# Masks of two attentions' logits written by VectorE instead of TensorE, with products of the side chains held behind the projections, in a two-layer mixer trunk

## The chip, the cores and the metric

One core of one Trainium2 chip runs the whole program. The metric is the device time of one execution in microseconds, as the median of several executions; the kernel before takes 605.12 us (three runs, 604.92 to 605.28). Engines are named as the profile names them: PE is TensorE's matrix multiplication, PEld its loads of the stationary operand, DVE is VectorE, ACT is ScalarE, POOL is GpSimd, SP issues the DMAs.

## What is computed

Two layers of a pre-norm mixer on 256 frames of width 1024. One wide projection feeds three token mixers: a gated linear attention (A), a sparse attention whose keys a token indexer picks (B), and a differential attention (C). Sigmoid gates merge them and an output projection adds the result to the residual stream. Cut to what matters:

```python
for l in range(DEPTH):                                    # 2 layers, T = 256, D = 1024
    h = rms(x, norm_g[l])
    gq, gk, gv, ga, gz, bq, bk, bv, iq, ik, iw, bz, cq, ck, cv, cz, gate = split(h @ w_in[l])
    y_a = gla(gq, gk, gv, ga, ...) * silu(gz)
    # B: score = sum_h iw[h] * relu(iq[h] . ik); the 64 best admissible keys of each query are kept
    #    p = softmax(where(kept, q . k, -inf)); o = p @ v
    y_b = dsa(bq, bk, bv, iq, ik, iw, ...) * silu(bz)
    # C: two maps a head; a query sees the keys up to the end of its chunk of 64 frames
    #    p_c = softmax(where(allowed, q_c . k_c, -inf)); o = (p_0 - lam * p_1) @ v
    y_c = diff(cq, ck, cv, ...) * silu(cz)
    g = sigmoid(gate.reshape(B, T, 3, D))
    x = x + (g0 * (y_a @ w_br[0]) + g1 * (y_b @ w_br[1]) + g2 * (y_c @ w_br[2])) @ w_out[l]
```

## The kernel before

Every product in float32 precision is made of three products of a high and a low part (`mm3`, L191 to L194: high by high, high by low, low by high). Weights arrive in units of 128 x 1024 (`raw`, five buffers); ACT rounds a unit to its high part `whi` and DVE subtracts to the low part `wlo` (L148; six buffers of each). The projections are the bulk of PE's work: for each name of `ORDER` (`bq`, `cq`, `ck`, `gate2`, ... `br0`, `gate5`, `gate1`, `br1`, `out..`) eight blocks of 128 rows of weights go into two accumulators of 128 x 512, one for each half `t` of the frames, out of a pool of four (`pj`, PSUM).

Between the blocks `flow.pump()` advances the side chains: generators, each started when the projections it needs are there, that yield a number of pumps to wait (table `Y`). Their accumulators come from a second pool of four PSUM banks (`at`). The chains that the change touches:

- `diff_task(t)` (mixer C). For each pair of maps it makes logits `clog`, a group of `per` heads by `S = 128 (t+1)` keys, always 128 x 512. Ahead of the products, L687 multiplies two bfloat16 constants (`rowsb`, `colsb`) into the accumulator: -1e30 for the first 64 queries on the last 64 keys. The products (L692, L693) add to it. Then DVE takes the negated maximum `negm` (L694), ACT the exponentials `cp` (L592), and later PE transposes the probabilities (`pT`) and multiplies by the values (`av`). There are six such groups a layer.
- `dsa_task` (mixer B): `dsa_index(t)` makes the scores on PE (`dots`), relu on ACT, the weighted sum `acc` on DVE, then eight rounds of maximum and replacement on DVE, and the mask `ns` of the keys not kept (DVE, then a POOL memset L588 of one corner). `dsa_attend(t)` multiplies `negi` (-1e30 times the identity, bfloat16) by `ns` into the logits `blog` (L620), adds the products, then `negm` (L624), exponentials `bp` (L592), transposes (L639) into `bpT`; `dsa_out` multiplies by the values (`av`), then `yb` (DVE), `ybh` and `ybl`. Three groups a layer.
- `gla_task` (mixer A): `state` products, ACT's `carry` copies (L801, L802) and the high part `Sh` (L205), DVE's `Sl`, then the products `go`.

The instruction order within an engine is made at build by a scheduler that places the traced instructions on a modelled timeline; each engine then executes its own list strictly in order. In the kernel before, a product of a chain may be placed ahead of projection products that were traced before it. Across engines semaphores hold an instruction until its inputs, or the buffer it writes, are free.

Of the kernel before, what the change touches and what calls it, by code (L numbers as in the profile page):

```python
# [10 lines left out]
BF16 = mybir.dt.bfloat16  # L11
AF = mybir.ActivationFunctionType
OP = mybir.AluOpType
# [3 lines left out]
L, T, D, BR = 2, 256, 1024, 512  # L17
NB = 3
P = 128
NOSYNC = mybir.DependencyInfo(mybir.DependencyClass.NoSync, mybir.DependencyReason.DATA)  # L20
# [6 lines left out]
NEG = -1e30  # L27
# [3 lines left out]
COL = dict(gq=0, gk=256, gv=512, ga=1024, gz=1040, bq=1552, bk=2064, bv=2576, iq=3088, ik=3600,  # L31
           iw=3664, bz=3672, cq=4184, ck=4696, cv=5208, cz=5720, gate=6232)
ORDER = ["bq", "cq", "ck", "gate2", "cz", "bk", "cv", "gq", "iq", "bv", "gv", "gz", "bz", "gate0", "gate3",
         "gate4", "br0", "gate5", "gate1", "br1", "out00", "out10", "out01", "out11"]
BRANCHES = (0, 2, 1)
UNIT, NUNIT = {}, 0
for _c in ORDER:
# [5 lines left out]
def columns(*widths):  # L43
    at, res = 0, {}
    for name, w in widths:
# [10 lines left out]
MERGE_WAIT = 4  # L56
WARM = 14
AHEAD1 = (0, 2)
Y = dict(sm0=0, qk0=1, qk=3, dsa0=6, dec0=8, diff0=1, gla0=0, att0=3, top=1, blog=2, bpT=11, by=6, clog=4,
         cpT=2, cy=2, za=17, q2=5, st=27, go=9)  # L60
BUFS = dict(w2=6, kp=25, w4=6, ev=2, raw=5, wt=6, ahead=21)


@with_exitstack
def trunk(ctx: ExitStack, tc: tile.TileContext, x0, x1, units, wsmall, pack, ptmp, wa2b, out):
    nc = tc.nc
    V, A, G, TE = nc.vector, nc.scalar, nc.gpsimd, nc.tensor

    cp = ctx.enter_context(tc.tile_pool(name="cp", bufs=1))
    wp = ctx.enter_context(tc.tile_pool(name="wp", bufs=1))  # L70
# [38 lines left out]
    ident, gT = xe[:, D:D + P], xe[:, D + P:]  # L109
# [52 lines left out]
    class Flow:  # L162
# [10 lines left out]
        def pump(self):  # L173
            for task in list(self.tasks):
                if not task[1] <= self.done:
                    continue
                if task[0] > 0:
                    task[0] -= 1
                    continue
                try:  # L180
                    task[0] = next(task[2]) - 1
                except StopIteration:
                    self.tasks.remove(task)

        def until(self, marks):
            while not marks <= self.done:
# [139 lines left out]


    m01 = cp.tile([P, 2, P], F32R, name="m01")
    negi = cp.tile([P, P], BF16, name="negi")
    rowsb = cp.tile([P, P], BF16, name="rowsb")  # L330
    colsb = cp.tile([P, T], BF16, name="colsb")
    gains = cp.tile([P, 2 * L], F32, name="gains")
    nlam = cp.tile([P, L], F32, name="nlam")

    def constants():
        nc.sync.dma_start(pk, pack)
        pt = w4([P, NPT], F32, "pt")
        nc.sync.dma_start(pt, ptmp)
        wa = w2([P, L, 256], F32, "wa")
        nc.sync.dma_start(wa, wa2b)  # L340
        A.activation(wah, wa, AF.Copy)
        V.tensor_sub(wal, wa, wah.bitcast(F32))
        A.activation(m01[:, 0], ptc(pt, "m0"), AF.Copy)
        A.activation(m01[:, 1], ptc(pt, "m1"), AF.Copy)
        A.activation(negi, ident, AF.Copy, scale=NEG)
        G.memset(rowsb[:, :64], 1.0)
        G.memset(rowsb[:, 64:], 0.0)
        G.memset(colsb[:, :T - 64], 0.0)
        G.memset(colsb[:, T - 64:], NEG)
        V.tensor_scalar_mul(gains[:, :L], pkc("qg"), 1.0 / math.sqrt(128.0))  # L350
        V.tensor_scalar_mul(gains[:, L:], pkc("dqg"), 0.125)
        for l in range(L):
            li = 0.8 - 0.6 * math.exp(-0.3 * l)
            e = tiny(2, "lame")
            for i in range(2):
                pr = sp.tile([P, 64], F32, tag="lamp", bufs=2, name=nm("lamp"))
                s = tiny(1, "lams")
                V.tensor_mul(pr, ptc(pt, "lam", (l * 4 + 2 * i) * 64, (l * 4 + 2 * i + 1) * 64),
                             ptc(pt, "lam", (l * 4 + 2 * i + 1) * 64, (l * 4 + 2 * i + 2) * 64))
                V.tensor_reduce(s, pr, axis=AX, op=OP.add)  # L360
                A.activation(e[:, i:i + 1], s, AF.Exp)
            d = tiny(1, "lamd")
            V.tensor_sub(d, e[:, 1:2], e[:, 0:1])
            V.tensor_scalar_add(nlam[:, l:l + 1], d, -li)
# [4 lines left out]
    ps = pj([P, CH], "idle")  # L369
# [11 lines left out]
    last = {}  # L381
# [7 lines left out]
    wt = [ws.tiles() for _ in range(4)]  # L389
# [60 lines left out]
    for l in range(L):  # L450
# [10 lines left out]
        bkT = (w4([P, 4, T], F32R, "bkh"), w4([P, 4, T], F32R, "bkl"))  # L461
        tts = [slice(t * P, t * P + P) for t in range(2)]

        def cq_task(mark, ps, dst):
            n = headnorm(ps, 8, 64)
            yield Y["qk"]
            ps, gain = transposed(n), gains[:, L + l:L + l + 1]
# [7 lines left out]
        def ck_task(mark, ps, tt):  # L475
            n = headnorm(ps, 8, 64)
            yield Y["qk"]
            ps, gain = transposed(n), pkc("dkg", l, l + 1)
# [7 lines left out]
        def qk_task(mark, ps, nh, dh, gain, hi, lo):  # L486
            n = headnorm(ps, nh, dh)
            yield Y["qk"]
            qkT(n, gain, hi, lo)
# [123 lines left out]
        def dsa_attend(t):  # L613
            S = (t + 1) * P
            per = CH // S
            sums, negm = tiny(4, "sums"), tiny(4, "negm")
            pT, prob = {}, {}
            for h0 in range(0, 4, per):
                ps = at([P, per, S], "blog")
                TE.matmul(ps, negi, notsel[t][:, :S].unsqueeze(1).to_broadcast([P, per, S]), start=True, stop=False)  # L620
                for j in range(per):
                    mm3(ps[:, j], bqT[t][0][:, h0 + j], bqT[t][1][:, h0 + j], bkT[0][:, h0 + j, :S],
                        bkT[1][:, h0 + j, :S], False, j == per - 1)
                V.tensor_reduce(negm[:, h0:h0 + per], ps, axis=AX, op=OP.max, negate=True)  # L624
                prob[h0] = w2([P, per, S], F32, "bp")
                for j in range(per):
                    softmax_rows(ps, j, S, prob[h0][:, j], negm, sums, h0 + j)
                yield 1
            rs = tiny(4, "rs")
            V.reciprocal(rs, sums)  # L630
            for h in range(4):
                p = prob[h // per * per][:, h % per]
                V.tensor_scalar_mul(p, p, rs[:, h:h + 1])
            yield Y["blog"]
            for h0 in range(0, 4, per):
                ps = at([P, per, t + 1, P], "pT")
                for j in range(per):
                    for s in range(t + 1):
                        TE.transpose(ps[:, j, s], prob[h0][:, j, s * P:(s + 1) * P], ident)  # L639
                hh = slice(h0, h0 + per)  # L640
                for s in range(t + 1):
                    hi, lo = (a[:, hh, tts[t]] if s == 0 else a[:, hh] for a in bpT[s])
                    A.activation(hi, ps[:, :, s], AF.Copy)
                    V.tensor_sub(lo, ps[:, :, s], hi.bitcast(F32))
                yield 1
            flow.done.add(f"bp{t}")
# [30 lines left out]
        def diff_task(t):  # L677
            S = (t + 1) * P
            per = CH // S
# [3 lines left out]
            for h0 in range(0, 4, per):  # L683
                for c in range(2):
                    i0 = c * 4 + h0
                    ps = at([P, per, S], "clog")
                    TE.matmul(ps, rowsb, colsb[:, T - S:].unsqueeze(1).to_broadcast([P, per, S]),  # L687
                              start=True, stop=False)
                    for j in range(per):
                        h = h0 + j  # L690
                        q = cqT[t][c]
                        TE.matmul(ps[:, j], q[:, h], ckT[c][:, h, :S], start=False, stop=False)  # L692
                        TE.matmul(ps[:, j], q[:, h], ckT[2 + c][:, h, :S], start=False, stop=j == per - 1)  # L693
                    V.tensor_reduce(negm[:, i0:i0 + per], ps, axis=AX, op=OP.max, negate=True)  # L694
                    p = w2([P, per, S], F32, "cp")
                    for j in range(per):
                        softmax_rows(ps, j, S, p[:, j], negm, sums, i0 + j)
                    prob[h0, c] = p
                    yield 1
                hh = slice(h0, h0 + per)  # L700
                r2 = tiny(4, "r2")
                V.reciprocal(r2[:, :per], sums[:, 4 + h0:4 + h0 + per])
                V.scalar_tensor_tensor(ratio[:, hh], r2[:, :per], nlam[:, l:l + 1], sums[:, hh],
                                       op0=OP.mult, op1=OP.mult)
                V.reciprocal(c1[:, hh], sums[:, hh])
                for j in range(per):
                    V.scalar_tensor_tensor(prob[h0, 0][:, j], prob[h0, 1][:, j], ratio[:, h0 + j:h0 + j + 1],
                                           prob[h0, 0][:, j], op0=OP.mult, op1=OP.add)
# [125 lines left out]
        notsel, val, th, mT = {}, {}, {}, {}  # L834
        bpT = [[w4([P, 4, T], F32R, "bpT") for _ in range(2)], [w2([P, 4, P], F32R, "bpT") for _ in range(2)]]
# [4 lines left out]
        ckT = [w4([P, 4, T], F32R, "ck") for _ in range(4)]  # L840
# [191 lines left out]
```

## Time and profile before

| | |
|---|---|
| median of three runs | 605.12 us |
| the profiled execution | 604.96 us |
| its span, first to last instruction | 603.2 us |
| PE busy | 596.3 us (99%) |
| DVE busy | 434.8 us (72%) |
| ACT busy | 350.8 us (58%) |
| POOL busy | 69.1 us (11%) |
| granted TensorE clock | 1.0 after the first microseconds |

A PE row's length is not its price: matmuls overlap in the pipeline, so a row of 128 x 512 is 0.39 us long while the next begins 0.23 us later. What a matmul costs the stream is read from start to start. Lines are those of the kernel printed above. The profile's chain of work that ended last puts 97% of the span on PE.

### The profile page before, as it was taken

The page shows a single profiled execution, that of the slowest core. Times are in us where ns is not written, and L with a number is a line of the kernel's source. Part 1 is how long each engine was busy: PE and PEld are TensorE (multiplying, and loading weights), DVE is VectorE, ACT ScalarE, POOL GpSimd, SP SyncE. Part 2 cuts the span into 40 slices and gives each one's busy share as a digit, 9 for nine tenths or more (in the row PEclk, how much of TensorE's full clock was granted, in tenths as well). Part 3 has the DMA queues.
Part 4 walks back from the last instruction along what each step waited for, and adds up shares of the span by engine and source line. Part 5 has one row for each costly group of instructions (what it writes and reads, how often), then busy time and mean ns, then how long its engine had stood idle before and what let it go on. Part 6 is the DMA issues. An engine that isn't in the chain of part 4 may idle for free.

```text
span 603.2 us, 8723 instructions
## 1 busy us (share of the span) xinstructions
PE 596.3 (99%) x3184; PEld 505.3 (84%) x3184; DVE 434.8 (72%) x713; ACT 350.8 (58%) x610; POOL 69.1 (11%) x99
## 2 busy tenths in 40 slices
PE   7999999999999999999999999999999999999997
PEld 4788888898898888888878888889888988888886
DVE  6978767877989756657587776676888986574661
ACT  5859956666546744443466787576754656535430
POOL 6034111000022000000010340201000120000000
PEclk9999999999999999999999999999999999999999
DMA  8764665335535645655546456532655165455601
GB/s 334 276 208 140 208 192 175 125 105 174 175 106 179 195 137 180 205 180 178 171 141 209 149 168 189 193 117 93 206 167 159 58 216 174 142 189 193 193 17 71
DMA packets 28267, 100.85 MB, mean 167 GB/s; under 512 B 3136, under 2 KB 3520, under 8 KB 28224
## 3 DMA queue, kind: packets, MB, share of 16 engines
q1 hardware_dynamic: 28224, 100.30, 50.7%
q8 instruction: 25, 0.41, 0.3%
q14 instruction: 18, 0.15, 0.1%
HBM read 99.23 MB, written 1.05 MB: 166 GB/s over the span
## 4 chain that ended last, share of the span: by engine, by line
PE 97%; DVE 1%; DMA 1%; ACT 1%; POOL 0%; issue 0%; SPq 0%
PE gate L192 7%; PE gate L194 7%; PE gate L193 7%; PE br L193 4%; PE br L192 4%; PE br L194 4%; PE out L194 2%; PE out L192 2%; PE out L193 2%; PE bz L194 1%; PE bz L192 1%; PE iq L193 1%; PE iq L192 1%; PE iq L194 1%; PE bz L193 1%; PE gv L192 1%
## 5 line engine op out<-in xcount | busy, mean ns | idle before, releaser
L148 DVE TENSOR_TENSOR wlo<-raw,whi 128x1024 fp32r<-128x1024 f32 x180 | 218.6, 1222 | 91.4 <-ACT whi L148 90.2
L148 ACT ACTIVATE whi<-raw 128x1024 fp32r<-128x1024 f32 x180 | 189.1, 1060 | 140.7 <-PE gate L194 38.0
L192 PE MATMUL gate<-whi,hTh 128*128 128x512 f32 x192 | 75.7, 394 | 0.0
L193 PE MATMUL gate<-wlo,hTh 128*128 128x512 f32 x192 | 75.2, 391 | 0.0
L194 PE MATMUL gate<-whi,hTl 128*128 128x512 f32 x192 | 75.1, 391 | 0.0
L194 PEld LDWEIGHTS gate<-whi,hTl 128*128 128x128 f32 x192 | 36.1, 188 | 7.3
L192 PEld LDWEIGHTS gate<-whi,hTh 128*128 128x128 f32 x192 | 36.1, 188 | 7.0
L193 PEld LDWEIGHTS gate<-wlo,hTh 128*128 128x128 f32 x192 | 36.1, 188 | 6.9
L199 POOL TENSOR_TENSOR r<-v,half 128x4 f32<-128x4 f32 (+1 forms) x24 | 36.9, 1539 | 2.0
L198 POOL TENSOR_SCALAR v<-ss 128x4 f32<-128x4 f32 (+1 forms) x24 | 9.1, 378 | 173.7 <-DVE ss L295 98.0
L192 PE MATMUL out<-whi,mTh 128*128 128x512 f32 (+1 forms) x72 | 26.7, 371 | 0.0
L193 PE MATMUL out<-wlo,mTh 128*128 128x512 f32 (+1 forms) x72 | 26.3, 366 | 0.0
L194 PE MATMUL out<-whi,mTl 128*128 128x512 f32 (+1 forms) x72 | 26.2, 366 | 0.0
L192 PE MATMUL br<-whi,yTh 128*128 128x512 f32 x64 | 24.9, 389 | 0.0
L193 PE MATMUL br<-wlo,yTh 128*128 128x512 f32 x64 | 24.9, 389 | 0.0
L194 PE MATMUL br<-whi,yTl 128*128 128x512 f32 x64 | 24.9, 389 | 0.0
L192 PE MATMUL iq<-hTh,whi 128*128 128x256 f32 x64 | 18.6, 290 | 0.0
L194 PE MATMUL bz<-hTh,wlo 128*128 128x256 f32 x64 | 18.3, 286 | 0.0
L193 PE MATMUL iq<-hTl,whi 128*128 128x256 f32 x64 | 18.2, 285 | 0.0
L192 PE MATMUL bz<-hTh,whi 128*128 128x256 f32 x64 | 18.2, 284 | 0.0
L194 PE MATMUL iq<-hTh,wlo 128*128 128x256 f32 x64 | 18.1, 282 | 0.0
L193 PE MATMUL bz<-hTl,whi 128*128 128x256 f32 x64 | 18.1, 282 | 0.0
(330 smaller groups left out, 1517.3 us busy)
## 6 DMA issues: line engine op xcount, KB each, us to landing
raw<-in_units SPq DMA_DIRECT2D x184, 512.0 KB, 3.4
wsr<-in_wsmall SPq DMA_DIRECT2D x2, 416.0 KB, 6.9
xe<-in_x SPq DMA_DIRECT2D x1, 584.0 KB, 3.5
x<-in_x SPq DMA_DIRECT2D x1, 512.0 KB, 7.9
out<-xe SPq DMA_DIRECT2D x2, 256.0 KB, 2.0
pt<-in_ptmp SPq DMA_DIRECT2D x1, 384.0 KB, 9.6
wa<-in_wa2b SPq DMA_DIRECT2D x1, 256.0 KB, 6.4
out<-x SPq DMA_DIRECT2D x1, 256.0 KB, 2.0
```

The lines of the kernel that those rows point to most:

```text
L148: self.splits[j] = (A.activation(hi, raw, AF.Copy), V.tensor_sub(lo, raw, hi.bitcast(F32)))
L192: TE.matmul(ps, lh, rh, start=first, stop=False)
L193: TE.matmul(ps, lh, rl, start=False, stop=False)
L194: TE.matmul(ps, ll, rh, start=False, stop=last)
L198: G.tensor_scalar(v, ss, 1.0 / dim, EPS, op0=OP.mult, op1=OP.add)
L199: G.tensor_tensor(r, v, half[:, :n], op=OP.pow)
```

## The change

- Mixer C: the mask product L687 goes; each head's products now start and end their own accumulation, and DVE then writes -1e30 with a `memset` into the masked corner (64 partitions, the last 64 keys of each head).
- Mixer B: the mask product L620 goes; after the products DVE multiplies `ns` by -1e30 and adds it to the logits in the accumulator with one `scalar_tensor_tensor` over 128 x 512.
- The constants `negi`, `rowsb`, `colsb`, with the ACT copy and four POOL memsets that made them, go.
- A wrapper around TensorE: a matmul or transpose that is issued from inside a chain gets an ordering edge (no semaphore) to the last one issued outside of chains, so that the scheduler may not place it ahead of projection products traced before it.
- `gate5` is projected before `br0`; `Y["blog"]` is 6 and not 2, `Y["by"]` 3 and not 6; `kp` has 27 buffers and not 25; the DMA scratch in SBUF is made smaller.

```diff
 ORDER = [..., "bz", "gate0", "gate3",
-         "gate4", "br0", "gate5", "gate1", "br1", "out00", "out10", "out01", "out11"]
+         "gate4", "gate5", "br0", "gate1", "br1", "out00", "out10", "out01", "out11"]
...
+    class Tensor:
+        chained, last = False, None
+        def put(self, i):
+            if not self.chained:
+                self.last = i
+            elif self.last is not None:
+                tc.add_manual_dep(i.ins, self.last.ins.name, NOSYNC, reason="order")
+            return i
+        def matmul(self, *a, **k):
+            return self.put(nc.tensor.matmul(*a, **k))
+        def transpose(self, *a, **k):
+            return self.put(nc.tensor.transpose(*a, **k))
...
     def pump(self):
...
+                TE.chained = True
                 try:
                     task[0] = next(task[2]) - 1
                 except StopIteration:
                     self.tasks.remove(task)
+                TE.chained = False
...
     def dsa_attend(t):
...
                 ps = at([P, per, S], "blog")
-                TE.matmul(ps, negi, notsel[t][:, :S].unsqueeze(1).to_broadcast([P, per, S]), start=True, stop=False)
                 for j in range(per):
                     mm3(ps[:, j], bqT[t][0][:, h0 + j], bqT[t][1][:, h0 + j], bkT[0][:, h0 + j, :S],
-                        bkT[1][:, h0 + j, :S], False, j == per - 1)
+                        bkT[1][:, h0 + j, :S], True, True)
+                V.scalar_tensor_tensor(ps, notsel[t][:, :S].unsqueeze(1).to_broadcast([P, per, S]), NEG, ps,
+                                       op0=OP.mult, op1=OP.add)
                 V.tensor_reduce(negm[:, h0:h0 + per], ps, axis=AX, op=OP.max, negate=True)
...
     def diff_task(t):
...
                     ps = at([P, per, S], "clog")
-                    TE.matmul(ps, rowsb, colsb[:, T - S:].unsqueeze(1).to_broadcast([P, per, S]),
-                              start=True, stop=False)
                     for j in range(per):
                         h = h0 + j
                         q = cqT[t][c]
-                        TE.matmul(ps[:, j], q[:, h], ckT[c][:, h, :S], start=False, stop=False)
-                        TE.matmul(ps[:, j], q[:, h], ckT[2 + c][:, h, :S], start=False, stop=j == per - 1)
+                        TE.matmul(ps[:, j], q[:, h], ckT[c][:, h, :S], start=True, stop=False)
+                        TE.matmul(ps[:, j], q[:, h], ckT[2 + c][:, h, :S], start=False, stop=True)
+                    V.memset(ps[0:64, :, S - 64:], NEG)
                     V.tensor_reduce(negm[:, i0:i0 + per], ps, axis=AX, op=OP.max, negate=True)
```

The programs' instruction lists show where things stand. First PE in layer 1, where the projection `gq` gives way to the first logits of mixer C; before:

```order
L194 MATMUL gq_1166<-whi_600,hTl 128x512
L687 LDWEIGHTS rowsb
L687 MATMUL clog_1189<-colsb,rowsb 128x512
L692 MATMUL clog_1189<-ck_239,cq_235 128x128
L693 MATMUL clog_1189<-ck_241,cq_235 128x128
```

and after (the wrapper's L82 stands for every product):

```order
L82 MATMUL gq_1158<-whi_592,hTh 128x512
L82 MATMUL gq_1158<-wlo_593,hTh 128x512
L82 MATMUL gq_1158<-whi_592,hTl 128x512
L82 MATMUL clog_1181<-ck_236,cq_232 128x128
L82 MATMUL clog_1181<-ck_238,cq_232 128x128
```

The group begins at the same block of `gq` as before, and the product over 512 columns ahead of it is gone. The whole PE list differs by 18 matmuls and their 18 loads: twelve of `clog`, six of `blog`; no other product is added or dropped.

Second, ACT in layer 1, from `gz`'s tanh (`th`) on: the exponentials `bp` of mixer B for the first half of the frames, and mixer A's `carry` and `Sh`. Before:

```order
L316 ACTIVATE th_2023<-gz_1854 128x512
L592 ACTIVATE bp_1968,sums_1951<-blog_1953,negm_1952 128x128 x4
L316 ACTIVATE th_2184<-bz_2029 128x512
L643 ACTIVATE bpT_231<-pT_2012 128x4x128
L801 ACTIVATE carry_2070<-state_2057 64x512
L802 ACTIVATE carry_2070<-state_2057 64x512
L205 ACTIVATE Sh_2073<-state_2057 128x512
```

After:

```order
L338 ACTIVATE th_2008<-gz_1846 128x512
L606 ACTIVATE bp_1960,sums_1943<-blog_1945,negm_1944 128x128 x4
L815 ACTIVATE carry_2055<-state_2042 64x512
L816 ACTIVATE carry_2055<-state_2042 64x512
L227 ACTIVATE Sh_2058<-state_2042 128x512
L338 ACTIVATE th_2176<-bz_2014 128x512
```

`carry` and `Sh` have moved up to stand right behind the exponentials; PE's `state` products, which they read, now stand earlier in PE's list, and the first `go` product, which reads `Sh`, as well.

Third, ACT in layer 1 at the end of mixer B: `ybh` is the high part of B's result, `gate_558` and `gate_559` (`gate_556` and `gate_557` after) are the accumulators of `gate3`, which the tanh frees. Before:

```order
L205 ACTIVATE ybh_2485<-yb_2483 128x512
L205 ACTIVATE yTh_2506<-yT_2501 128x512
L205 ACTIVATE ybh_2525<-yb_2523 128x512
L919 ACTIVATE gate_2535<-gate_558_2414 128x512
L919 ACTIVATE gate_2537<-gate_559_2415 128x512
```

After:

```order
L227 ACTIVATE ybh_2498<-yb_2496 128x512
L227 ACTIVATE ybh_2523<-yb_2521 128x512
L168 ACTIVATE whi_1982<-raw_1980 128x1024
L933 ACTIVATE gate_2527<-gate_556_2388 128x512
L933 ACTIVATE gate_2529<-gate_557_2389 128x512
```

A weight's split stands between `ybh` and the tanh now. On PE, 16 products of `gate4` over 512 columns stand between the last `av` product and the first of `gate5`, which writes the accumulator that this tanh frees; before, `br0` came there.

## Rows read from the trace of the kernel before

**Rows 1.** The page: busy time by engine; granted TensorE clock in 40 slices.

```profile
PE 596.3 (99%) x3184; PEld 505.3 (84%) x3184; DVE 434.8 (72%) x713; ACT 350.8 (58%) x610; POOL 69.1 (11%) x99
PEclk9999999999999999999999999999999999999999
```

**Rows 2.** PE's waits: who waited for whom, total us, times, longest us.

```profile
PE bq L193 <- DVE wlo L397: 1.3, 2, 0.7
...
PE qkT L305 <- DVE qn L298: 0.2, 1, 0.2
```

**Rows 3.** PE by line and shape: busy us, mean ns (mask products).

```profile
L687 PE MATMUL clog<-colsb,rowsb 128*128 128x512 bf16 x12 | 4.7, 391 | 0.0
...
L620 PE MATMUL blog<-ns,negi 128*128 128x512 bf16 x6 | 2.3, 390 | 0.0
```

**Rows 4.** PE's timeline (start us, length us), a mask ahead of 256-column products.

```profile
106.99 0.39 PE L687 MATMUL clog<-colsb,rowsb 128*128 128x512 bf16 x1
107.03 0.47 PE L692 MATMUL clog<-ck,cq 128*128 128x256 f32 x1
107.33 0.28 PE L693 MATMUL clog<-ck,cq 128*128 128x256 f32 x1
107.45 0.28 PE L692 MATMUL clog<-ck,cq 128*128 128x256 f32 x1
```

**Rows 5.** PE's timeline, a mask ahead of 128-column products.

```profile
100.24 0.39 PE L194 MATMUL gq<-whi,hTl 128*128 128x512 f32 x1
100.47 0.39 PE L687 MATMUL clog<-colsb,rowsb 128*128 128x512 bf16 x1
...
100.75 0.28 PE L693 MATMUL clog<-ck,cq 128*128 128x128 f32 x1
```

**Rows 6.** PE's timeline, 128-column products behind a 512-column projection, without a mask.

```profile
134.42 0.22 PE L194 MATMUL av<-cvh,pTl 128*128 128x128 f32 x1
134.48 0.28 PE L192 MATMUL av<-cvh,pTh 128*128 128x128 f32 x1
```

**Rows 7.** DVE and POOL by line and shape: busy us, mean ns.

```profile
L148 DVE TENSOR_TENSOR wlo<-raw,whi 128x1024 fp32r<-128x1024 f32 x180 | 218.6, 1222 | 91.4 <-ACT whi L148 90.2
...
L571 DVE SCALAR_TENSOR_TENSOR acc<-relu,iws,acc 128x128 f32<-128x128 f32 x14 | 4.9, 348 | 0.3
...
L660 DVE SCALAR_TENSOR_TENSOR yb<-av,bz 128x512 f32<-128x512 f32 x4 | 2.8, 688 | 1.0 <-PE av L194 1.0
...
L545 DVE TENSOR_TENSOR iqe<-iq,iqe 64x512 fp32r<-64x512 f32 x4 | 2.7, 684 | 0.1
...
L574 POOL MEMSET acc<- 64x64 f32 x4 | 0.6, 144 | 55.3 <-DVE acc L571 55.3
```

**Rows 8.** All engines' waits: the weights' rounding on ACT.

```profile
ACT whi L148 <- PE gate L194: 38.0, 26, 1.8
```

**Rows 9.** Timelines of PE, POOL and ACT: the sparse chain, layer 1.

```profile
144.75 0.31 PE L561 MATMUL dots<-ikh,iqe 128*128 128x128 f32 x1
...
166.91 0.14 POOL L588 MEMSET ns<- 64x64 bf16 x1 [0.32 <-DVE ns L587]
...
173.23 0.37 ACT L592 ACTIVATE bp<-blog,negm 128x128 f32<-128x128 f32 x1 [2.87 <-DVE negm L624]
...
174.52 0.21 ACT L592 ACTIVATION_READ_ACCUMULATOR bp<-blog,negm 128x1 f32 x1
...
180.99 0.60 ACT L205 ACTIVATE Sh<-state 128x512 fp32r<-128x512 f32 x1
...
183.58 0.22 PE L192 MATMUL go<-Sh,q2Th 128*128 128x128 f32 x1
```

**Rows 10.** Timelines of PE and ACT: the end of the sparse chain, layer 1.

```profile
215.93 0.27 PE L194 MATMUL av<-bpT,bvl 128*128 128x128 f32 x1
...
216.97 0.63 ACT L205 ACTIVATE ybh<-yb 128x512 fp32r<-128x512 f32 x1
217.51 1.07 ACT L919 ACTIVATE gate<-gate 128x512 f32<-128x512 f32 x2
```

More of the change, by code (lines that the diff above doesn't have):

```diff
@@ L58 @@
 AHEAD1 = (0, 2)
-Y = dict(sm0=0, qk0=1, qk=3, dsa0=6, dec0=8, diff0=1, gla0=0, att0=3, top=1, blog=2, bpT=11, by=6, clog=4,
+Y = dict(sm0=0, qk0=1, qk=3, dsa0=6, dec0=8, diff0=1, gla0=0, att0=3, top=1, blog=6, bpT=11, by=3, clog=4,
          cpT=2, cy=2, za=17, q2=5, st=27, go=9)
-BUFS = dict(w2=6, kp=25, w4=6, ev=2, raw=5, wt=6, ahead=21)
+BUFS = dict(w2=6, kp=27, w4=6, ev=2, raw=5, wt=6, ahead=21)
 @with_exitstack
@@ L66, in trunk @@
     nc = tc.nc
-    V, A, G, TE = nc.vector, nc.scalar, nc.gpsimd, nc.tensor
+    V, A, G = nc.vector, nc.scalar, nc.gpsimd
+    class Tensor:
[10 more added lines that the diff above has]
+            return self.put(nc.tensor.transpose(*a, **k))
+    TE = Tensor()
     cp = ctx.enter_context(tc.tile_pool(name="cp", bufs=1))
@@ L328, in trunk @@
     m01 = cp.tile([P, 2, P], F32R, name="m01")
-    negi = cp.tile([P, P], BF16, name="negi")
-    rowsb = cp.tile([P, P], BF16, name="rowsb")
-    colsb = cp.tile([P, T], BF16, name="colsb")
     gains = cp.tile([P, 2 * L], F32, name="gains")
@@ L344, in constants @@
         A.activation(m01[:, 1], ptc(pt, "m1"), AF.Copy)
[L345 to L349, printed above, removed]
         V.tensor_scalar_mul(gains[:, :L], pkc("qg"), 1.0 / math.sqrt(128.0))
@@ L1019 @@
     from concourse.bass_utils import run_bass_kernel_spmd as run
-    nc = bacc.Bacc("TRN2", target_bir_lowering=False, num_devices=1)
+    nc = bacc.Bacc("TRN2", target_bir_lowering=False, num_devices=1, dynamic_dma_scratch_size=4096)
     arrays, args = {}, []
```

## The prediction

> **What bounds the kernel now.** First the page's busy times and clock [rows 1]: PE is busy for 99% of the span and the granted clock reads 9, 90% or more of full speed, in every slice, so the upper of its two levels, so the end can come earlier only if PE's stream gets shorter. Busy PE is not PE at its peak, so the second view is PE's waits: four rows in all, 3.4 us together, of which the largest and the smallest stand in [rows 2]; nearly all lie in the first 17 us. Third, PE's timeline shows how the stream is priced. A 512-column product occupies a row of 0.39 us, but the next one starts 0.23 us later ([rows 5]: 100.24 to 100.47), and it does so in stretches with no wait. So PE is limited by the columns it streams, and every product that leaves the stream shortens the program by its start-to-start price, provided that no new wait arises.
>
> **The change part by part.** *The masks leave PE.* Eighteen mask products go: twelve `clog` and six `blog` [rows 3]. Their rows' 390 ns is not the price. Ahead of 256-column products, the mask and the first product take 107.33 - 106.99 = 0.34 us together, and such a product alone 107.45 - 107.33 = 0.12 us, so a mask costs 0.22 us [rows 4]. Ahead of 128-column products, mask and first product take 100.75 - 100.47 = 0.28 us [rows 5]; without a mask, the first 128-column product behind a wide projection takes 134.48 - 134.42 = 0.06 us [rows 6], again 0.22 us. Twelve masks are of the first kind and six of the second: 18 x 0.22 = 4.0 us. The masks' weight loads were hidden under the stream before them, and go at nothing.
>
> Weighed against a rule: the rows put 0.22 to 0.23 us on a 512-column product in an unbroken stream [rows 5]. The Trainium skill, page "TensorE: Matmul & The Clock Gate", section "Back-to-back issue gap", gives about 131 ns for such a product in a sustained stream with its weight load. By that figure 18 masks would be worth an estimated 2.4 us; the trace does not agree with it, and the sum here goes by the rows.
>
> *DVE takes the masks.* Six `scalar_tensor_tensor` over 128 x 512 in PSUM: priced by `yb`, which reads PSUM at the same size, 0.69 us each, 4.1 us. Twelve memsets of 64 partitions by 128 or 256 elements: no row of before has one in PSUM. The bounds are the 64 x 64 memset on POOL, 0.14 us, and a 64 x 512 pass of DVE, 0.68 us; I take the 128 x 128 pass, 0.35 us, which is nearest in elements, so 4.2 us (1.7 to 8.2) [rows 7]. DVE's busy time goes from 434.8 to some 443 us, 74%. The cover is DVE's and ACT's lead: the largest single wait of ACT's rounding is for PE to free a weight buffer (38.0 us in 26 waits [rows 8]), so weights are split ahead of need. If the cover were gone, each memset or mask would cost PE its own 0.35 or 0.69 us. The ACT copy and four POOL memsets that made the constants ran in the first 25 us and released nothing that PE waited for: nothing.
>
> *Pinned products.* The ordering edges add no semaphore. They hold chain products back, so PE meets them later, with more time for their inputs; what they delay is the work behind them. Two places could turn that into a PE wait.
>
> (a) `Sh` ahead of `go`. In the sparse chain of before, `dots` starts at 144.75 and `ns` starts its last step at 166.91 and ends 0.14 later, 22.3 us after `dots`; `go` starts 38.8 us after `dots` [rows 9]. In the changed lists PE has 16 products of 512 columns fewer, one of 256 more and three of 128 fewer between the first `dots` and the first `go`: -16 x 0.227 + 0.12 - 3 x 0.11 = -3.8 us, so `go` comes 35.0 us after `dots`. Between the first step of `acc` and `ns`, DVE's list has eight more instructions: two `wlo` (1.22 us each [rows 7]) and six that I price at 0.69 at most, together 6.6 us. `ns` is then there 28.9 us after `dots`. Now DVE's mask waits for `ns`, and behind it on ACT stand the exponentials `bp`, `carry` and `Sh`, in that order. The path adds the mask 0.69, `negm` 0.68 (a pass of the same size as `yb`), four exponentials (173.23 to 174.73, 1.5 us) and three ACT passes of 0.6 us as `Sh` [rows 9]: 4.7 us. `Sh` is ready at 33.6 us, `go` due at 35.0: cover 1.4 us, on a price that is an upper one. So no wait, but not much to spare, and it recurs in layer 2.
>
> (b) `gate5` behind `gate3`'s tanh, layer 1. From the last `av` product to the end of `ybh` were 216.97 + 0.63 - 215.93 = 1.7 us [rows 10]; now a weight's rounding (1.06 us, as ACT's others of 128 x 1024) and one tanh (1.07 for two, so 0.54 [rows 10]) follow ahead of the release: 3.3 us. PE has 16 products, 16 x 0.227 = 3.6 us, and the last `av` itself, 0.1. Cover 0.4 us: likely no wait, and an overrun costs its own length once.
>
> *The other waits.* `Y["blog"]` and `Y["by"]` shift where B's transposes and values are traced; B's result is needed by the third branch of `br0`, which `gate5` ahead of it delays by 48 products, 10.9 us, so the shift is covered. The total of products stays, and SP's transfers are as many, in the order of need that ORDER gives. Two more `kp` buffers hold gates longer; no row of PE waits for them.
>
> *Sum.* The profiled execution took 604.96 us, span 603.2 and 1.8 around it, and lies 0.16 under the median of the runs shown. 604.96 - 4.0 = 600.96; against the median 605.12 - 4.0 = **601.1 us**.
>
> **The rivals.** *Small new waits.* The covers of 0.4 us in (b) and 1.4 us twice in (a) are differences of two long sums; if hardware eats them by up to 1 us each, 0.5 to 2 us come back, 601.6 to 603.1, say 602.2. For: DVE is the busiest helper and gets 8 us more. Against: PE's waits of before are almost nil with covers of the same kind.
>
> *A mask hid a load.* PE's weight loads are busy 505.3 us for 3184, 0.16 us each [rows 1]. If each mask's stream covered one load of the products behind it, and that load shows once the mask is gone, a mask is worth 0.22 - 0.16 = 0.06 us, all of them 1.1 us: 604.0. For: loads are busy 84% of the span. Against: the 0.06 us of [rows 6], where a narrow product stands behind a wide one with no mask and no load shows. The skill's figure above is another price below that of the rows; the time by it would be an estimated 602.7.
>
> *The masks' time is waited out instead.* If `go` waits for `Sh` in each layer as long as that layer's nine masks took, 2.0 us, nothing changes: 605.1. It needs the path of (a) 1.4 + 2.0 = 3.4 us later than reckoned.
>
> *Slower.* The same loop, further: PE's `go` waits for ACT's `Sh`, ACT for `bp`, DVE's mask for `ns`, and DVE's own queue of weight splits stands in front of `ns`; while ACT waits, it rounds no weights. From 3.4 us of lateness a layer the kernel is slower than before, from 4.0 by more than 0.2%. At 5 us late it is 601.1 + 2 x (5 - 1.4) = 608.3. For: ACT's list is strictly ordered and `Sh` now stands right behind the exponentials. Against: 6.6 us for the added DVE work is already an upper price, and idle time of DVE before (waits for ACT) absorbs some of it.
>
> **How the numbers follow.** 0.2%, 1.2 us, is about what a measurement of this kernel can tell from no change: faster means under 603.9, slower over 606.3. Forecast as summed 0.72; small new waits 0.15; a hidden load each 0.03; waited out 0.06; slower 0.04. The first two are faster: 0.87. The next two lie within 0.2%: 0.09. Slower 0.04. The range starts at 600.5: below the forecast if masks are 0.227 each (4.1), if `qkT`'s 0.2 us wait [rows 2] goes with the ACT copy, and by the runs' scatter of 0.2. It ends at 602.8, which takes in most of the small waits, and leaves some 0.15 out.
>
> **What would show it.** Right: no bfloat16 products but the warm-up's on PE, PE's spacing unchanged, span near 599.2, PE's waits still 3 to 4 us in the first 20, mask passes of DVE near 0.69 us. Wrong: a PE wait of `go` for ACT `Sh` or DVE `Sl` near 180 and 475 us, of `gate` for ACT's tanh near 222 us, or of projections for `wlo`; or the clock below 1.0 behind such a wait. The forecast fails if these waits exceed 1.5 us in sum, or if a memset in PSUM takes far longer than 0.7 us.

## The result, and the profile after

The changed kernel takes 601.78 us (median of six runs, 601.70 to 602.97) against 605.12 us; the ratio is 0.9949, 95% interval 0.9939 to 0.9959. That is 3.34 us less. The forecast was 4.0 us less, 601.1, with a range of 600.5 to 602.8. The profiled execution took 601.70 us, with a span of 599.8 us.

The page of the changed kernel, busy time by engine and the granted clock, answers to [rows 1]:

```profile
PE 593.6 (99%) x3166; PEld 504.4 (84%) x3166; DVE 438.6 (73%) x731; ACT 348.8 (58%) x609; POOL 66.5 (11%) x95
...
PEclk9999999999999999999999999999999999999999
```

PE lost 18 products and 2.7 us of busy time, DVE gained 18 instructions and 3.8 us, and PE is still the bound. PE's waits in the changed kernel (who waited for whom, total us, times, longest us) answer to [rows 2]:

```profile
PE bq L82 <- DVE wlo L411: 1.3, 2, 0.7
PE idle L82 <- DVE idle L382: 1.2, 1, 1.2
PE qkT L85 <- DVE qn L320: 0.2, 1, 0.2
```

No new wait has come, neither of `go`, `gate` or `av` nor of a projection. The `hps` row of 0.7 us that the page of before had isn't there, but nothing is gained by that: `hps` starts at 6.46 us, before at 6.48. The same stretch as in [rows 5] on PE's timeline after the change (start us, length us; products that write and read the same tiles are put together in one row, which shows the shape of the first):

```profile
100.19 0.39 PE L82 MATMUL gq<-whi,hTl 128*128 128x512 f32 x1
100.42 1.53 PE L82 MATMUL clog<-ck,cq 128*128 128x128 f32 x12
101.79 0.40 PE L82 MATMUL gq<-whi,hTh 128*128 128x512 f32 x1
```

The logits now begin where the mask stood in [rows 5], and from the wide product ahead of them to the first `clog` product there are 0.23 us, the full price of a wide product. Behind it stand eight products over 128 columns and four over 256, which take 1.37 us (100.42 to 101.79). The eight take 0.84 us, 0.11 or less each (the first of the four starts at 101.26): no weight load shows although the mask's stream no longer covers it. The kernel before had the same twelve products with two masks between 100.47 and the next `gq` product:

```profile
101.54 0.39 PE L687 MATMUL clog<-colsb,rowsb 128*128 128x512 bf16 x1
...
102.24 0.40 PE L192 MATMUL gq<-whi,hTh 128*128 128x512 f32 x1
```

That is 1.77 us, 0.40 more for two masks.

What DVE pays is in its groups by shape (busy us, mean ns), beside [rows 7]:

```profile
L637 DVE SCALAR_TENSOR_TENSOR blog<-ns,blog 128x512 f32<-128x512 bf16 x6 | 3.9, 684 | 0.0
...
L707 DVE MEMSET clog<- 64x128 f32 x8 | 1.3, 165 | 1.2 <-PE clog L82 1.0
L707 DVE MEMSET clog<- 64x256 f32 x4 | 1.1, 272 | 1.6 <-PE clog L82 1.5
```

The mask in B is 684 ns (forecast 0.69 us), the memset in C 165 or 272 ns (forecast 0.35, between 0.14 and 0.68). Together their rows are 6.3 us long and not 8.3; DVE's busy time grew by 3.8 only: rows of neighbouring instructions overlap, and the eight rows that scale B's probabilities over 128 x 128 became shorter (mean 552 ns before, 279 after), which was not traced further.

### The profile page after: what moved, and what is told of

Same layout as the page of the kernel before. It is cut to its first block, busy times and chain, and to the rows that moved or that the text cites. A ratio compares the mean times of both kernels' runs of the same rounds, so it can differ in the third digit from the quotient of the medians.

```text
span 599.8 us, 8713 instructions
## 1 busy us (share of the span) xinstructions
PE 593.6 (99%) x3166; PEld 504.4 (84%) x3166; DVE 438.6 (73%) x731; ACT 348.8 (58%) x609; POOL 66.5 (11%) x95
## 4 chain that ended last, share of the span: by engine, by line
PE 97%; DVE 1%; DMA 1%; ACT 1%; POOL 0%; issue 0%; SPq 0%
PE gate L82 22%; PE br L82 11%; PE out L82 7%; PE bz L82 4%; PE iq L82 4%; PE gz L82 4%; PE cz L82 4%; PE gv L82 4%; PE gq L82 4%; PE ck L82 4%; PE cv L82 4%; PE bv L82 4%; PE bk L82 4%; PE bq L82 3%; PE cq L82 3%; PE av L82 2%
## 5 line engine op out<-in xcount | busy, mean ns | idle before, releaser
L82 PE MATMUL gate<-whi,hTh 128*128 128x512 f32 x192 | 75.5, 394 | 0.0
L82 PE MATMUL gate<-wlo,hTh 128*128 128x512 f32 x192 | 75.3, 392 | 0.0
L82 PE MATMUL gate<-whi,hTl 128*128 128x512 f32 x192 | 75.3, 392 | 0.0
L82 PEld LDWEIGHTS gate<-whi,hTl 128*128 128x128 f32 x192 | 36.1, 188 | 7.2
L82 PEld LDWEIGHTS gate<-wlo,hTh 128*128 128x128 f32 x192 | 36.1, 188 | 7.1
L82 PEld LDWEIGHTS gate<-whi,hTh 128*128 128x128 f32 x192 | 36.1, 188 | 6.9
L221 POOL TENSOR_TENSOR r<-v,half 128x4 f32<-128x4 f32 (+1 forms) x24 | 34.2, 1426 | 2.0
L82 PE MATMUL out<-whi,mTh 128*128 128x512 f32 (+1 forms) x72 | 26.7, 371 | 0.0
L82 PE MATMUL out<-wlo,mTh 128*128 128x512 f32 (+1 forms) x72 | 26.3, 366 | 0.0
L82 PE MATMUL out<-whi,mTl 128*128 128x512 f32 (+1 forms) x72 | 26.2, 366 | 0.0
L82 PE MATMUL br<-whi,yTh 128*128 128x512 f32 x64 | 24.9, 389 | 0.0
L82 PE MATMUL br<-wlo,yTh 128*128 128x512 f32 x64 | 24.9, 389 | 0.0
L82 PE MATMUL br<-whi,yTl 128*128 128x512 f32 x64 | 24.9, 389 | 0.0
L82 PE MATMUL iq<-hTh,whi 128*128 128x256 f32 x64 | 18.7, 292 | 0.0
L82 PE MATMUL iq<-hTl,whi 128*128 128x256 f32 x64 | 18.4, 288 | 0.0
L82 PE MATMUL bz<-hTh,whi 128*128 128x256 f32 x64 | 18.4, 287 | 0.0
L82 PE MATMUL iq<-hTh,wlo 128*128 128x256 f32 x64 | 18.3, 287 | 0.0
L82 PE MATMUL bz<-hTl,whi 128*128 128x256 f32 x64 | 18.2, 285 | 0.0
L82 PE MATMUL bz<-hTh,wlo 128*128 128x256 f32 x64 | 18.1, 283 | 0.0
```

Of the source, the lines that this page charges most:

```text
L82: return self.put(nc.tensor.matmul(*a, **k))
L221: G.tensor_tensor(r, v, half[:, :n], op=OP.pow)
```

## The experiments

All times are medians in us. The kernel before was run beside each group: 605.26 beside the first four, 605.10 beside the next four, 605.16 beside the last three.

| run | what it has | us | ratio, 95% interval |
|---|---|---|---|
| e1 | masks on DVE, all else as before | 604.72 | 0.9995, 0.9986 to 1.0004 |
| e2 | all else of the change, masks on PE | 605.18 | 0.9997, 0.9989 to 1.0006 |
| e3 | the change without ordering edges | 601.97 | 0.9946, 0.9933 to 0.9960 |
| e4 | before, with each mask product twice | 609.18 | 1.0063, 1.0051 to 1.0076 |
| e5 | e1 with `Y["blog"]` 6 | 602.07 | 0.9955, 0.9942 to 0.9969 |
| e6 | the change with `Y["blog"]` 2 | 605.40 | 1.0004, 0.9995 to 1.0012 |
| e7 | the change, B's mask pass three times | 609.65 | 1.0074, 1.0061 to 1.0086 |
| e8 | the change, no mask anywhere | 601.66 | 0.9944, 0.9931 to 0.9956 |
| e9 | before, B's masks alone on DVE | 604.01 | 0.9983, 0.9974 to 0.9992 |
| e10 | before, C's masks alone on DVE | 608.15 | 1.0045, 1.0033 to 1.0058 |
| e11 | before, no mask anywhere | 601.13 | 0.9932, 0.9919 to 0.9944 |

### What the two halves of the change do alone

e1 is the kernel before with only the masks moved:

```diff
-                TE.matmul(ps, negi, notsel[t]..., start=True, stop=False)
...
+                V.scalar_tensor_tensor(ps, notsel[t]..., NEG, ps, op0=OP.mult, op1=OP.add)
...
-                    TE.matmul(ps, rowsb, colsb[:, T - S:]..., start=True, stop=False)
...
+                    V.memset(ps[0:64, :, S - 64:], NEG)
```

> The kernel before with only the masks moved to DVE: no ordering edges, the old order of names, the old waits and buffers. Theory A (the gain is the 18 mask products and nothing else of the change matters): 601.8 us, as the changed kernel, PE's waits unchanged. Theory B (the other edits are the cover that keeps the later, DVE-masked sparse chain off PE): PE waits for ACT at av and at gate4 near 209 and 503 us, 1 to 1.5 us a layer, 603.5 to 604.6 us.

Measured: 604.72 us, no difference from before that can be told, 0.1 above the range of theory B. Of the 4 us only half a microsecond arrived. Two PE waits had come, each once a layer, of `av` for ACT's `bpT` and of `gate` for ACT's tanh:

```profile
PE av L192 <- ACT bpT L636: 1.2, 2, 0.6
...
PE gate L192 <- ACT gate L911: 0.8, 2, 0.4
```

e2 is the complement: edges, `ORDER`, `Y` and buffers as in the changed kernel, masks on PE.

> The changed kernel with the masks back on PE: ordering edges, new waits, order and buffers stay. Theory A and B: 605.1 us plus what the other order costs in PE's stream. If the 0.7 us that the changed kernel lacks of the summed 4.0 come from the ordering edges, it takes 605.5 us or more; if they come from the masks' own price or from the products left behind, 605.1.

Measured: 605.18 us, nothing gained and nothing lost that can be told; of the two cases in the expectation that is the second, so the 0.7 us that the changed kernel lacks of 4.0 are not seen in the other edits by themselves. So neither half does anything alone, and together they give 3.3 us: one half is the cover that the other needs. e3 takes one part of that half away again, the edges:

```diff
-            elif self.last is not None:
-                tc.add_manual_dep(i.ins, self.last.ins.name, NOSYNC, reason="order")
```

> The changed kernel without the ordering edges, all else as in it. If the edges carry part of the gain (cover), PE gets a new wait and it takes over 602.3 us; if they cost stream time, 601.4; if they do nothing of weight, 601.8.

Measured: 601.97 us, 0.2 above the changed kernel, no more than runs scatter. The pinned products carry no weight that can be told.

### What a mask is worth on PE

e4 is the kernel before and writes each mask product a second time into the accumulator (of `clog` and `blog` alike); nothing else of it changes:

```diff
+                    TE.matmul(ps, rowsb, colsb[:, T - S:]..., start=False, stop=False)
```

> The kernel before with each of the 18 mask products issued twice; the second adds the same -1e30 again. It measures the price of a mask in the stream: at 0.22 us each 605.1 + 4.0 = 609.1 us; at 0.13 us each (the Trainium skill's sustained figure) 607.5; if a mask hid weight loads, the second one costs its full 0.227, 609.2, while its removal gains less.

Measured: 609.18, 3.92 above the kernel before beside it (605.26): 18 more products, 0.218 us each. e11 goes the other way and takes all masks out of the kernel before, with the constants that they used; nothing is put in their place (`Y["blog"]` stays 2):

> The kernel before with all masks left out on PE and none on DVE (the softmaxes of B and C run over keys that should be excluded), Y["blog"] 2, ORDER and buffers of before. Theory 1 (PE, being 4 us shorter, simply meets B's transposes too early): the waits of av and gate come up without any DVE mask, 604 to 605. Theory 2 (the DVE masks in B's and C's chains make B late): no new waits, 601.2 to 601.6.

Measured: 601.13, 4.03 below before, 0.224 us a mask. So the forecast's main term, 18 x 0.22 = 4.0 us, holds in both directions. Theory 1 of that expectation, that a shorter PE stream alone makes PE meet B's products too early, is not borne out: e11 shows no new wait. It is no clean test, though, for in e11 the build places B's chain itself earlier than before (see e10).

### Which number is the cover

e5 adds a single number to e1:

```diff
-Y = dict(..., blog=2, bpT=11, by=6, ...)
+Y = dict(..., blog=6, bpT=11, by=6, ...)
```

> The kernel before with the masks on DVE and one number more, Y["blog"] 6 for 2; ORDER, Y["by"], the buffers and the unpinned order stay as before. Theory 1 (the later logits of mixer B are what covers the moved masks; the other edits carry nothing): the waits of av and gate that the masks alone showed are gone, and the time is that of the changed kernel, 601.8 to 602.1 us, ratio 0.9945. Theory 2 (gate5 ahead of br0, or the earlier values, gives the cover): the waits stay, 604.5 to 604.9, ratio 0.999.

Measured: 602.07 us. One number brings back 2.7 us of e1's loss (2.5 if each is taken against the kernel before beside it); `ORDER`, `Y["by"]`, the buffers and the edges are then worth some 0.3 us together, no more than runs scatter. e6 is the reverse, the changed kernel with that number alone put back to 2:

> The changed kernel with Y["blog"] back at 2 alone; pinned products, ORDER, Y["by"] and buffers are those of the changed kernel. Theory 1 (this number is the cover): PE waits of av for ACT's bpT and of gate for ACT's tanh come up near 209 and 503 us, some 2.8 us in sum, and the time is 604.4 to 604.9 us, ratio 0.999. Theory 2 (another edit is the cover): 601.8 to 602.1, PE's waits as in the changed kernel.

Measured: 605.40, 0.5 above theory 1's range, and 3.6 above the changed kernel. PE's waits of e6:

```profile
PE gate L82 <- ACT gate L933: 1.0, 2, 0.6
PE av L82 <- ACT bpT L658: 0.6, 1, 0.6
...
PE pT L85 <- DVE bp L648: 0.5, 1, 0.5
```

They sum to 2.1 us, less than the 3.6 lost. A wait row counts from the modelled end of the product ahead, while PE could have started the next one before that end, so start to start more is lost than the row says. The timelines of e6 (DVE, ACT and PE) show the place in layer 1; of its last two rows, `av` to `gate` is 1.01 us where a 256-column product alone takes 0.12 [rows 4], so 0.89 us are lost where the row says 0.63:

```profile
210.35 0.87 DVE L648 TENSOR_SCALAR bp<-bp,rs 128x256 f32<-128x256 f32 x3
...
211.23 0.91 ACT L658 ACTIVATE bpT<-pT 128x256 fp32r<-128x256 f32 x2
212.04 1.08 ACT L933 ACTIVATE gate<-gate 128x512 f32<-128x512 f32 x2
...
210.76 0.96 PE L85 MATMUL pT<-xe,bp 128*128 128x128 f32 x6 [0.47 <-DVE bp L648]
211.67 0.39 PE L82 MATMUL av<-bpT,bvh 128*128 128x256 f32 x1
212.68 0.50 PE L82 MATMUL gate<-whi,hTh 128*128 128x512 f32 x1 [0.63 <-ACT gate L933]
```

PE wants to transpose B's probabilities of the second half of the frames while DVE still scales them (to 211.22). ACT's `bpT` and, behind it in ACT's list, the tanh that frees an accumulator for `gate4` are late in turn. The changed kernel at the same place:

```profile
207.75 0.87 DVE L648 TENSOR_SCALAR bp<-bp,rs 128x256 f32<-128x256 f32 x3
...
206.73 1.11 ACT L933 ACTIVATE gate<-gate 128x512 f32<-128x512 f32 x2
...
212.32 0.82 PE L85 MATMUL pT<-xe,bp 128*128 128x128 f32 x6
```

Here DVE is done 3.7 us before the six transposes, and the tanh stands ahead of `bpT`, 5.3 us earlier. `Y["blog"]` is the number of pumps between the scaling of B's probabilities and their transposes: 6 pumps cover what 2 don't. The number acts on both lists: the six transposes start 1.6 us later than in e6, and DVE's scaling in front of them ends 2.6 us earlier.

### Whose masks make B late

e9 moves B's six masks alone to DVE, e10 C's twelve alone; everything else is as before (in e10 the constants of C's masks go with them).

> The kernel before with mixer B's six masks alone on DVE; mixer C's twelve stay products on PE, and Y, ORDER and buffers are those of before. Theory 1 (the masks-alone kernel waits because B's own chain got a DVE pass longer): the waits of av for bpT and of gate for tanh come up here too, up to 2.9 us, and the time is 604.9 to 606.5. Theory 2 (a mask in B's chain is covered; the waits come with C's): no such waits, 6 x 0.22 = 1.3 us less, 603.8.

> The kernel before with mixer C's twelve masks alone on DVE; B's six stay products on PE, Y, ORDER and buffers of before. Theory 1 (the waits come from B's longer chain): no new PE wait, 12 x 0.22 = 2.6 us less, 602.5. Theory 2 (C's masks make them: PE reaches B's transposes earlier, or DVE's memsets stand ahead of B's steps in DVE's list): waits of av and gate near 210 and 505 us, 1.5 us or more a layer, 604.5 to 606.8.

Measured: e9 604.01, 1.15 below before, 0.19 us a mask and no new wait, near theory 2's 603.8; e10 608.15, 3.0 above before and 1.4 above the range of its theory 2. So the longer chain of B (theory 1 of e9) isn't it: the DVE pass in B costs nothing that can be told, and it is the memsets in C that bring the waits. PE's new waits in e10:

```profile
PE bz L192 <- DVE gvl L206: 1.3, 2, 0.7
PE av L192 <- ACT bpT L637: 1.3, 2, 0.7
...
PE gate L192 <- ACT gate L912: 0.8, 2, 0.4
```

Two of them are those of e1. The third, of `bz` for DVE's `gvl` (the low part of mixer A's values, near 176 and 472 us), no theory had named.

How B lags is seen at its first `dots` and at the mask `ns` of its second half. In e10 (timelines of PE and DVE):

```profile
147.25 0.30 PE L555 MATMUL dots<-ikh,iqe 128*128 128x128 f32 x1
...
198.90 0.28 DVE L581 TENSOR_TENSOR ns<-ns,nf 128x256 bf16<-128x256 bf16 x1
```

Before, `dots` began at 144.75 [rows 9], and the second half's `ns` stood here:

```profile
192.81 0.28 DVE L587 TENSOR_TENSOR ns<-ns,nf 128x256 bf16<-128x256 bf16 x1
```

In e11, where nothing is masked:

```profile
143.53 0.31 PE L553 MATMUL dots<-ikh,iqe 128*128 128x128 f32 x1
...
183.41 0.29 DVE L579 TENSOR_TENSOR ns<-ns,nf 128x256 bf16<-128x256 bf16 x1
```

So against the kernel before, C's memsets alone put `dots` 2.5 us and this `ns` 6.1 us later. The six memsets of a layer are 1.2 us of DVE, and those of layer 1 are over by 114 us, 33 us ahead of `dots`; as time on DVE they can't make the lag. The order of the lists shows more: between the first `acc` and the first half's `ns` DVE has 6 `wlo` before and in e11, but 8 in e10; up to the second half's `ns` it has 13 before, 8 in e11 and 15 in e10, each 1.23 us long, so 2 x 1.23 = 2.5 us more than before. On PE, masks not counted, 749 products stand ahead of the first `dots` before and in e11, and 763 in e10. The same 763 stand there in every kernel with the memsets on DVE (e1, e3, e5, e6, e7 and the changed kernel), and 749 in every one without (e2, e4, e8, e9). So the build's scheduler, with the memsets on DVE, places B's steps later in the lists. That much is read from lists and traces; why its model does so was not tried, and how much of the 6.1 us each of these changes of order makes was not separated.

### What DVE's passes cost in the changed kernel

e8 leaves all masks out of the changed kernel:

```diff
-                V.scalar_tensor_tensor(ps, notsel[t]..., NEG, ps, op0=OP.mult, op1=OP.add)
...
-                    V.memset(ps[0:64, :, S - 64:], NEG)
```

> The changed kernel without any mask: both masks are left out, on PE and on DVE, so the softmaxes of mixers B and C run over keys that should be excluded. Theory 1 (DVE's 18 masks lie wholly beside PE's stream): the time of the changed kernel within 0.3 us, 601.5 to 602.0, the small rest by how many times PE changes between wide and narrow products. Theory 2 (they cost a part of the 0.7 us that the forecast missed): 601.1 to 601.3.

Measured: 601.66 us, 3.44 below before; the changed kernel is 3.34 below. With the cover in place DVE's 18 instructions cost some 0.1 us, no more than runs scatter.

e7 makes B later than the changed kernel has it:

```diff
                 V.scalar_tensor_tensor(ps, notsel[t]..., NEG, ps, op0=OP.mult, op1=OP.add)
+                V.scalar_tensor_tensor(ps, notsel[t]..., 0.0, ps, op0=OP.mult, op1=OP.add)
+                V.scalar_tensor_tensor(ps, notsel[t]..., 0.0, ps, op0=OP.mult, op1=OP.add)
```

> The changed kernel with two more DVE passes on each group of B's logits (the mask again, times 0.0, so the values stay), 0.68 us each, so the second half's chain, with two groups, is 2.7 us later, and the first half's 1.4. Theory 1 (the changed kernel's cover at gate5's accumulator is some 0.7 us, and at go 2.3): a PE wait of gate for ACT comes up near 224 and 518 us, 1 to 2.1 us each, none of go; 604 to 606 us, ratio 0.998 to 1.002. Theory 2 (the sparse chain has slack enough everywhere): 601.8 to 602.1, ratio 0.9945. Theory 3 (go is the tight place, as the prediction's slower rival has it): a PE wait of go near 182 and 477.

Measured: 609.65, slower than before and above every theory's time. The place and the length of the wait are those of theory 1. PE's waits in e7:

```profile
PE gate L82 <- ACT gate L937: 4.2, 2, 2.1
```

PE's timeline around the first of them:

```profile
225.02 0.27 PE L82 MATMUL av<-bpT,bvl 128*128 128x128 f32 x1
227.36 0.61 PE L82 MATMUL gate<-whi,hTh 128*128 128x512 f32 x1 [2.06 <-ACT gate L937]
227.76 0.63 PE L82 MATMUL gate<-wlo,hTh 128*128 128x512 f32 x1
...
231.11 0.39 PE L82 MATMUL gate<-whi,hTh 128*128 128x512 f32 x1
```

With B later, the build has put the last `av` right ahead of `gate5`; the 16 products of `gate4` that stood between them in the changed kernel now stand earlier, and the whole loop `av`, `yb`, `ybh`, tanh lies open. Then comes what no theory had: the products behind the wait are 0.43 us apart and not 0.23. The windows of e7 around it (stretch, length, then busy us of each engine, granted clock, DMA share, GB/s):

```profile
core 0: us, PE busy (x) PEld busy (x) DVE busy (x) ACT busy (x) POOL busy (x), PEclk, DMA share, GB/s
200.00:226.00 26.00, 25.30 (x132) 21.43 (x130) 23.04 (x39) 16.07 (x35) 1.20 (x2) 1.00 0.53 174
226.00:228.00 2.00, 0.64 (x2) 0.53 (x3) 1.45 (x3) 2.00 (x5) 0.00 (x0) 0.90 0.72 252
228.00:231.00 3.00, 3.00 (x8) 2.35 (x8) 0.00 (x0) 0.77 (x2) 0.00 (x0) 0.50 0.00 0
231.00:236.00 5.00, 5.00 (x23) 4.13 (x23) 0.00 (x0) 0.78 (x1) 0.00 (x0) 1.00 0.00 0
```

From 228 to 231 us the granted clock is 0.50, the lower level. The sum: the wait is 227.36 - 225.02 - 0.11 = 2.23 us start to start, and nine products of 512 columns take 3.75 us (227.36 to 231.11) where nine at 0.227 take 2.04, 1.71 us more. Twice 3.94 is 7.9 of the 8.1 us by which e7's span of 607.9 exceeds the changed kernel's 599.8.

## Why the prediction was right, and where it fell short

**The masks' price, 18 x 0.22 = 4.0 us: right.** Taking them out gave 4.03 (e11), doubling them cost 3.92 (e4 against the kernel before). The rival of a load hidden by the mask (0.06 us a mask) falls with the same runs. The Trainium skill's figure, page "TensorE: Matmul & The Clock Gate", section "Back-to-back issue gap" (about 131 ns for such a product), would have given an estimated 2.4 us; e4 and e11 do not agree with it.

**The 0.7 us that were missed: open.** They aren't a PE wait, and DVE's work is some 0.1 of them (e8). The rest, 0.5 to 0.6, lies between e11 (4.03 below before) and e8 (3.44 below), both without masks. The profiles agree in sign and put it at 0.3 us (spans of 599.4 and 599.7), spread over start-up and B's stretch of each layer. That would lay it on the other edits, which the forecast set at nothing by "the total of products stays". But e2, with these same edits and the masks on PE, is no slower than before (605.18 against 605.26); e5, which has `Y["blog"]` alone of them, comes no nearer to 4.0 (3.0 below before); and the 95% intervals of e8 and e11 overlap. So the cause isn't shown. One candidate doesn't explain it: the times that PE changes from products of 256 or 512 columns to narrower ones are 73 in e11 and 74 in e8.

**DVE's prices.** The pass in B was right to 0.01 us. The memset was mis-sized, 0.35 against 0.17 and 0.27 us, inside its bounds; it hung on rows of other operations. Nothing followed from it, as DVE isn't the bound.

**(a), cover at `go`: right.** The changed kernel's timelines (PE, POOL, DVE, ACT) answer to [rows 9]:

```profile
146.84 0.30 PE L82 MATMUL dots<-ikh,iqe 128*128 128x128 f32 x1
...
174.72 0.14 POOL L602 MEMSET ns<- 64x64 bf16 x1 [0.85 <-DVE ns L601]
...
174.93 0.68 DVE L637 SCALAR_TENSOR_TENSOR blog<-ns,blog 128x512 f32<-128x512 bf16 x1
175.65 0.69 DVE L639 TENSOR_REDUCE negm<-blog 128x4 f32<-128x512 f32 x1
...
176.37 0.37 ACT L606 ACTIVATE bp<-blog,negm 128x128 f32<-128x128 f32 x1 [5.87 <-DVE negm L639]
...
179.12 0.60 ACT L227 ACTIVATE Sh<-state 128x512 fp32r<-128x512 f32 x1
...
181.98 0.23 PE L82 MATMUL go<-Sh,q2Th 128*128 128x128 f32 x1
```

From `dots`, `ns` is there after 28.0 us (forecast 28.9), `Sh` after 32.9 (33.6), and `go` starts after 35.1 (35.0). The cover is 2.3 us where 1.4 was reckoned; the path from `ns` to `Sh` took 4.9 us (4.7).

**(b), cover at `gate5`: right.** The timelines of PE and ACT answer to [rows 10]; PE's `gate` row is the 17th product behind the last `av`, the first of `gate5`:

```profile
221.03 0.27 PE L82 MATMUL av<-bpT,bvl 128*128 128x128 f32 x1
...
222.07 0.64 ACT L227 ACTIVATE ybh<-yb 128x512 fp32r<-128x512 f32 x1 [0.63 <-DVE yb L675]
...
223.56 1.55 ACT L933 ACTIVATE gate<-gate 128x512 f32<-128x512 f32 x3
...
224.84 0.39 PE L82 MATMUL gate<-whi,hTh 128*128 128x512 f32 x1
```

The first of the three tanh ends near 224.08 (a third of 1.55 us), 0.8 us before the product that needs its accumulator; 0.4 had been reckoned.

**The step that failed: "The other waits", and with it the choice of the two places in "Pinned products".** The forecast looked for the danger in the pinned products, at `go` and at `gate5`, and called `Y["blog"]` a shift that is covered. The danger came from the moved masks themselves, C's memsets above all (e10), at a place that the forecast didn't reckon: B's second half, where the scaled probabilities meet their transposes (e6). There the masks alone wait back 2.9 to 3.6 us, and that one number is what removes it (e5, e6). So the number came out right with a term of some 3 us missing on either side: a loss by lateness, and its cure. In the list of the changed kernel the cure had already been at work, which is why the covers read from that list were right. That no wait arose at the place which the forecast did not reckon was luck.

**The slower rival** had a true mechanism, a late B that PE waits for, and e10 shows it 3 us slower than before with C's masks alone. Its places were `gate`, `av` and `bz`, not `go`; and its price, one for one, was too low where the clock falls (e7).

## What to carry to other kernels

Work that leaves a bound engine is worth its start-to-start price, and that can be read from a few rows; whether the price arrives is decided by the chains on the engine that takes the work. So reckon the lateness of every later meeting of that engine with the bound one, not only of the meetings that the diff touches, and take a one-number edit in a table of waits as seriously as the visible edit beside it: here it held some 2.7 of the 3.3 us (e5 against e1). A part that shows nothing when tried alone (e2) can be what the rest depends on.

## What the runs showed of the hardware

Behind a PE wait of 2.06 us in e7 the wide products that start between 227.36 and 231.11 us are 0.36 to 0.43 us apart, at the lower clock level, and the same follows the second wait, of 2.10 us: the wait cost 2.2 us and the clock 1.7 more. Single waits of 0.4 to 0.75 us, in e6 and e10, were followed by no fall (granted clock 1.0). The Trainium skill, page "TensorE: Matmul & The Clock Gate", section "What's actually happening", tells that the array has these two levels and that its recent activity sets which one is granted; e7's windows, 1.00, then 0.50, then 1.00, agree.

DVE writes a corner of 64 partitions in PSUM in 165 ns for 128 elements a partition and 272 ns for 256, some 0.8 ns an element more from one to the other; a pass over 128 x 512 in PSUM with a second operand takes 684 ns.
